# The last column chunk of a trunk's final GEMM cut into 384 and 128 tokens, the short piece in two feature halves

## The chip, the core and the metric

One core of a Trainium2 chip runs the kernel. Its engines work side by side, each in its own program order: TensorE (PE: matrix products into PSUM banks; PEld is its weight load), VectorE (DVE), ScalarE (ACT), GpSimd (POOL) and SyncE (SP), which here issues the DMAs. An instruction waits on semaphores for what it needs, and everything behind it on its engine or queue waits with it. The metric is device time in microseconds. A difference is told from no change when it is over 0.2%.

## The reference

Two layers run on 512 tokens of 2048 features in float32, a pooling mixer and then a sparse attention, each with adaLN shift, scale and gate; then one RMSNorm. What matters here is the end of layer 1 and what follows it:

```
mod = cond @ mod_w[i] + mod_b[i]
shift, scale, gate = jnp.split(mod, 3, axis=-1)
h = rms_norm(x, norm_g[i]) * (1.0 + scale[:, None, :]) + shift[:, None, :]
...
return (o * jax.nn.silu(gate)) @ w_out      # dsa_branch: output projection, 2048 x 2048
...
x = x + gate[:, None, :] * out
return rms_norm(x, final_g)                 # mean of squares over all 2048 features of a token
```

A token can only be normalised when all of its 2048 output features exist.

## The kernel before, in words

Activations are kept with features on the 128 partitions and tokens along the free dimension: a GEMM makes 128 features by up to 512 tokens in one PSUM bank. Each float32 product is made of three matmuls on fp32r halves: weight high by activation high, weight high by activation low, weight low by activation high (lines 191 to 193).

Weights come in units. `unit` (lines 143 to 151) has SP load a unit of 256 input rows by 512 output features into `st` (512 KB, three buffers), ACT cast it to the high half `wh` (L148, three buffers), and DVE subtract to get the low half `wl` (L150, three buffers). A `st` buffer comes free when its subtraction is done, a `wh` or `wl` buffer when TensorE has used it. `next_unit` keeps up to three units begun ahead of use, in the order of the list `plan`.

`gemm_t` (L178) goes over eight units (2048 input rows); for each it goes over four blocks of 128 features, two halves of the unit's rows, and the three products, so 24 matmuls a unit and 192 for a 512-feature chunk. In the last unit it calls `evac` for each block. After each unit it may run a hook (`mid`) and takes one item of the list `hot`.

The last GEMM (layer 1's `wout1`) has four chunks of 512 features. Chunks 0 to 2 take all 512 tokens at once. The last chunk is done in two pieces of tokens, 0 to 255 and 256 to 511, each with its own pass over the chunk's eight units (lines 1026 and 1027; line 977 lists them twice). The evacuation `out_evac` (L479 to L486) loads the residual `xr` (two buffers), forms the new `x2` on DVE (L481), squares it on ACT (L294), adds the square to `acc` on DVE (L295), and scales `x2` by `final_g` on ACT (L486). `norm_r` (L262) sums `acc` over the partitions with one-column matmuls (L266), and makes the reciprocal root (L269 to L280; the root on ACT, L271, loads an ACT table the first time). `fin_item` (L1005) then turns 128 tokens by 1024 features with eight TensorE transposes (L1013) into two banks, scales one bank on ACT (L1016) and the other on DVE (L1018), and has SP store both, 256 KB each (L1020; eight `fin` buffers). Eight items make the output: four for each token piece.

PSUM has eight banks: four named `acc`, three `att` and one `misc`; `bank()` (L90) deals out the first two names in turn. A scheduler lays the program's instructions out for each engine, mostly in program order; how they stand there is shown below.

Of the kernel before, what the change touches and what calls it, by code (L numbers as in the profile page):

```python
# [18 lines left out]
T = 512  # L19
# [33 lines left out]
def trunk(ctx, tc, xT, cols, crow, pos, modT, win, wgrp, wout0, widx, wgate, wqkv, wout1, out):  # L53
# [65 lines left out]
    hot = deque()  # L119
# [36 lines left out]
    plan = [(win[c, kp], 512) for k0, k1 in groups for c in chunks for kp in range(k0, k1)]  # L156
# [18 lines left out]
        nc.vector.tensor_tensor(lo, src, hi.bitcast(F32), op=OP.subtract)  # L175


    def gemm_t(kps, rhs, new_bank, evac, t0=0, t1=T, nstep=1, nhot=1, mid={}):  # L178
        banks = []
        for n, kp in enumerate(kps):  # L180
            wh, wl = next_unit()
            for m in range(4):
                if n == 0:
                    banks.append(new_bank())
                o = banks[m][:, 0:t1 - t0]
                for kk in range(2):
                    rh, rl = rhs(2 * kp + kk)
                    ms = slice(m * 128, m * 128 + 128)
                    first = n == 0 and kk == 0
                    last = n == len(kps) - 1 and kk == 1  # L190
                    mm(o, wh[:, kk, ms], rh[:, t0:t1], start=first, stop=False)  # L191
                    mm(o, wh[:, kk, ms], rl[:, t0:t1], start=False, stop=False)  # L192
                    mm(o, wl[:, kk, ms], rh[:, t0:t1], start=False, stop=last)  # L193
                if n == len(kps) - 1:
                    evac(m, o)
            if n in mid:
                mid[n]()
            step(nstep, nhot)
# [63 lines left out]
    def norm_r(t0, t1):  # L262
        nb = (t1 - t0) // 128
        p = misc()
        for j in range(nb):
            mm(p[:, j:j + 1], P["acc"][:, t0 + j * 128:t0 + j * 128 + 128], ones[:, 0:1], start=True, stop=True)  # L266
        s = P["tp"].tile([128, 4, 4], F32, name="nrm", tag="nrm", bufs=2)
        v, r, u, iv = (s[:, a, 0:nb] for a in range(4))
        nc.vector.tensor_scalar(v, p[:, 0:nb], 1.0 / D, EPS, op0=OP.mult, op1=OP.add)  # L269
        nc.vector.reciprocal(iv, v)  # L270
        nc.scalar.activation(r, iv, AF.Sqrt)  # L271
        refine(r, u, v)
        return r
# [177 lines left out]
    yT = {}  # L451
    while hot:
        hot.popleft()()
    for g in range(4):
        pooled = {}
        for kk in range(4):
            k = 4 * g + kk
# [14 lines left out]
    def out_evac(i, c, t0, t1, keep):  # L472
        def evac(m, o):
            mt = 4 * c + m
            if ("g", i, mt) not in done:
                ensure(("g", i, mt))
            xr = P["tp"].tile([128, T], F32, name="xr", tag="xr", bufs=2)
            n = t1 - t0
            nc.sync.dma_start(xr[:, 0:n], (xT if i == 0 else x1d)[mt][:, t0:t1])  # L479
            dst = keep(mt, t0, t1)  # L480
            nc.vector.scalar_tensor_tensor(dst, o, Gc[:, i, mt:mt + 1], xr[:, 0:n], op0=OP.mult, op1=OP.add)  # L481
            if i == 0:
                nc.sync.dma_start(x1d[mt][:, t0:t1], dst)
            add_square(dst, t0, t1, mt == 0)
            if i == 1:
                nc.scalar.activation(dst, dst, AF.Copy, scale=fg[:, mt:mt + 1])  # L486
        return evac
# [37 lines left out]
    for t0, hooks in ((0, {}), (256, {0: a0, 2: b0})):  # L525
        for c in (2, 3):
            gemm_t(range(8), lambda k: yT[k], bank, out_evac(0, c, t0, t0 + 256, keep0), t0, t0 + 256,
                   nstep=0, nhot=NH0, mid=hooks if c == 2 else {})
    early, early_g = [], []
    gemm_t(range(8), lambda k: hT[k], bank, lambda m, o: early_g.append((m, o)), 0, 256, nstep=0, nhot=NH1,  # L530
           mid={0: a1, 2: b1_})
# [383 lines left out]
    yT = {}  # L915
# [58 lines left out]
    eq.close()  # L974
    ctx.enter_context(open_banks())
    ctx.enter_context(open_work("right"))
    plan += [(wout1[c, kp], 512) for c in (0, 1, 2, 3, 3) for kp in range(8)]
    gemm_t(range(8), lambda k: yT[k], bank4, lambda m, o: early.append((m, o)), nstep=2.6, nhot=2, mid={6: drain})
    drain()
    el.close()  # L980
# [17 lines left out]
        gemm_t(range(8), lambda k: yT[k], bank, out_evac(1, c, 0, T, keep1), nstep=1)  # L998
    fin = {}

    def fin_r(t0):
        fin[t0] = norm_r(t0, t0 + 256)


    def fin_item(t0, tt, hf):  # L1005
        def run():
            r = fin[t0]
            c0 = t0 + tt * 128
            for q in range(2):
                p = bank()  # L1010
                for kk in range(4):
                    k = 8 * hf + 4 * q + kk
                    nc.tensor.transpose(p[:, kk * 128:kk * 128 + 128], x2[k][:, c0:c0 + 128], ident)  # L1013
                f = op_.tile([128, 512], F32, name="fin", tag="fin", bufs=8)
                if q == 0:
                    nc.scalar.activation(f, p, AF.Copy, scale=r[:, tt:tt + 1])  # L1016
                else:
                    nc.vector.tensor_scalar(f, p, r[:, tt:tt + 1], None, op0=OP.mult)  # L1018
                f0 = hf * 1024 + q * 512
                nc.sync.dma_start(out[c0:c0 + 128, f0:f0 + 512], f)  # L1020
        return run

    def fin_items(t0):
        return [fin_item(t0, tt, hf) for tt in range(2) for hf in range(2)]

    gemm_t(range(8), lambda k: yT[k], bank, out_evac(1, 3, 0, 256, keep1), 0, 256, nstep=0)
    gemm_t(range(8), lambda k: yT[k], bank, out_evac(1, 3, 256, T, keep1), 256, T, nstep=0,
           mid={0: lambda: fin_r(0), 2: lambda: hot.extend(fin_items(0))})
    fin_r(256)
    hot.extend(fin_items(256))  # L1030
    drain()
    es.close()

# [46 lines left out]
```

## Time and profile before

| | |
|---|---|
| median of 3 runs | 1649.99 us (1649.84 to 1651.13) |
| profiled execution, its own time | 1649.42 us |
| its span, first to last instruction | 1647.7 us |
| TensorE busy in the span | 98% |
| granted TensorE clock, mean over the span | 0.998 |
| last chunk, tokens 0 to 255 | 1584.36 to 1606.12 us |
| last chunk, tokens 256 to 511 | 1606.12 to about 1632.28 us |
| from there to the end of the span | 15.4 us |

The profiled execution's own time is 1.7 us longer than its span. Times of rows are microseconds from the start of the span. A matmul's row begins when it starts; matmuls are pipelined, so the distance between two starts, and not the length of a row, is what one costs. DMA rows on SPq are issues; the data lands later.

### The profile page before, as it was taken

The numbers are of one execution on the slowest core, as the hardware profiler recorded it, in microseconds if no ns is written. First come the engines' busy times: TensorE is split into PE (matmuls) and PEld (weight loads), VectorE is DVE, ScalarE is ACT, GpSimd is POOL, SyncE is SP. The second block draws the span as 40 slices with busy tenths as digits, with TensorE's granted clock in tenths as the row PEclk, the third lists the DMA queues.
The fourth block names the chain that finished last, engine by engine and source line by source line (L and its number), as shares of the span: only waits on it lengthen the run. The fifth ranks groups of instructions, "written<-read, shape, count | busy, mean of one in ns | idle before, by whom it ended". The sixth has DMA issues, their size and how long they took to land.

```text
span 1647.7 us, 23827 instructions
## 1 busy us (share of the span) xinstructions
PE 1615.6 (98%) x8892; PEld 1458.4 (89%) x8892; DVE 1259.6 (76%) x2147; ACT 726.4 (44%) x1150; POOL 128.0 (8%) x238
## 2 busy tenths in 40 slices
PE   5999999999999999999999999999999999999997
PEld 3888888888889999998889999999999999988897
DVE  6899999999974689765796676667776777756864
ACT  5622221334323556453324555455545555544344
POOL 0000000000000000010002121121312213000000
PEclk9999999999999999999999999999999999999999
DMA  9888888543786776442347897886968778637954
GB/s 347 318 302 308 322 336 339 207 178 114 289 294 207 237 246 195 142 148 100 104 152 170 196 175 165 181 166 176 168 169 179 166 185 163 201 115 279 363 183 171
DMA packets 106533, 348.21 MB, mean 211 GB/s; under 512 B 11953, under 2 KB 20273, under 8 KB 94001
## 3 DMA queue, kind: packets, MB, share of 16 engines
q1 hardware_dynamic: 87986, 296.35, 51.4%
q0 software_dynamic: 18432, 50.34, 18.3%
q8 instruction: 70, 1.15, 0.3%
q14 instruction: 45, 0.37, 0.1%
HBM read 330.39 MB, written 16.25 MB: 210 GB/s over the span
## 4 chain that ended last, share of the span: by engine, by line
PE 88%; DVE 4%; issue 3%; DMA 2%; ACT 1%; POOL 1%; SPq 0%; DVEq 0%; POOLq 0%; ACTq 0%
PE acc L191 11%; PE acc L192 11%; PE acc L193 11%; PE att L192 6%; PE att L191 6%; PE att L193 6%; PE by L816 4%; PE by L817 4%; PE by L818 4%; PE bx L816 2%; PE bx L818 2%; PE bx L817 2%; PE bz L816 2%; PE bz L818 2%; PE bz L817 2%
## 5 line engine op out<-in xcount | busy, mean ns | idle before, releaser
L148 ACT CAST wh<-st 128x1024 fp32r<-128x1024 f32 (+1 forms) x232 | 236.1, 1018 | 489.8 <-PE acc L192 266.3
L150 DVE TENSOR_TENSOR wl<-st,wh 128x1024 fp32r<-128x1024 f32 (+1 forms) x232 | 274.0, 1181 | 143.9 <-ACT wh L148 141.3
L191 PE MATMUL acc<-hi,wh 128*128 128x512 f32 (+1 forms) x810 | 299.0, 370 | 0.0
L192 PE MATMUL acc<-lo,wh 128*128 128x512 f32 (+1 forms) x810 | 298.9, 369 | 0.0
L193 PE MATMUL acc<-hi,wl 128*128 128x512 f32 (+1 forms) x810 | 298.5, 369 | 0.0
L226 DVE SCALAR_TENSOR_TENSOR ms<-ms,cb 128x2048 f32<-128x2048 f32 x96 | 218.9, 2285 | 12.3 <-DMA ms<-modT 10.1
L192 PEld LDWEIGHTS acc<-lo,wh 128*128 128x128 f32 x810 | 152.7, 189 | 26.6 <-DVE lo L175 0.2
L191 PEld LDWEIGHTS acc<-hi,wh 128*128 128x128 f32 x810 | 152.6, 189 | 26.5 <-ACT hi L174 0.4
L193 PEld LDWEIGHTS acc<-hi,wl 128*128 128x128 f32 x810 | 152.5, 188 | 26.5 <-DVE wl L150 0.2
L175 DVE TENSOR_TENSOR qwl<-qx,qwh 128x768 fp32r<-128x768 f32 x128 | 122.0, 957 | 66.8 <-ACT qwh L174 64.2
L191 PE MATMUL att<-hi,wh 128*128 128x512 f32 (+1 forms) x406 | 148.2, 366 | 4.7 <-ACT hi L311 4.7
L174 ACT CAST qwh<-qx 128x768 fp32r<-128x768 f32 x128 | 106.7, 836 | 102.7 <-PE bz L818 37.3
L192 PE MATMUL att<-lo,wh 128*128 128x512 f32 (+1 forms) x406 | 148.5, 366 | 0.0
L193 PE MATMUL att<-hi,wl 128*128 128x512 f32 (+1 forms) x406 | 148.3, 365 | 0.0
L175 DVE TENSOR_TENSOR qwl<-qy,qwh 128x768 fp32r<-128x768 f32 x96 | 91.5, 956 | 50.6 <-ACT qwh L174 48.8
L174 ACT CAST qwh<-qy 128x768 fp32r<-128x768 f32 x96 | 79.8, 833 | 88.1 <-PE by L818 39.2
L741 POOL DMA_DIRECT2D qx<-wqkv x96 | 83.4, 872 | 433.8 <-DVE stt L870 199.5
L191 PEld LDWEIGHTS att<-hi,wh 128*128 128x128 f32 x406 | 76.5, 189 | 17.5 <-ACT hi L311 5.1
L816 PE MATMUL bx<-qwh,hi 128*128 128x384 f32 x256 | 89.1, 348 | 0.0
L192 PEld LDWEIGHTS att<-lo,wh 128*128 128x128 f32 x406 | 76.6, 189 | 13.4 <-DVE lo L312 0.7
L816 PE MATMUL by<-qwh,hi 128*128 128x384 f32 x256 | 88.1, 344 | 0.0
L193 PEld LDWEIGHTS att<-hi,wl 128*128 128x128 f32 x406 | 76.7, 189 | 12.5
(286 smaller groups left out, 3501.1 us busy)
## 6 DMA issues: line engine op xcount, KB each, us to landing
ms<-modT SPq DMA_DIRECT2D x96, 1024.0 KB, 6.8
st<-wout SPq DMA_DIRECT2D x88, 512.0 KB, 4.1
qx<-wqkv POOLq DMA_DIRECT2D x96, 384.0 KB, 5.9
st<-win SPq DMA_DIRECT2D x64, 512.0 KB, 4.8
qy<-wqkv SPq DMA_DIRECT2D x64, 384.0 KB, 3.5
st<-wgate SPq DMA_DIRECT2D x40, 512.0 KB, 3.5
qx<-wqkv SPq DMA_DIRECT2D x32, 384.0 KB, 3.5
qy<-wqkv POOLq DMA_DIRECT2D x32, 384.0 KB, 5.9
```

Source lines behind the costliest of these rows:

```text
L148: nc.scalar.copy(wh, st)
L150: nc.vector.tensor_tensor(wl, st, wh.bitcast(F32), op=OP.subtract)
L174: nc.scalar.copy(hi, src)
L175: nc.vector.tensor_tensor(lo, src, hi.bitcast(F32), op=OP.subtract)
L191: mm(o, wh[:, kk, ms], rh[:, t0:t1], start=first, stop=False)
L192: mm(o, wh[:, kk, ms], rl[:, t0:t1], start=False, stop=False)
L193: mm(o, wl[:, kk, ms], rh[:, t0:t1], start=False, stop=last)
L226: nc.vector.scalar_tensor_tensor(st, st, 1.0, cell["cb"], op0=OP.mult, op1=OP.mult, accum_out=dst)
L741: nc.gpsimd.dma_start(d[kp], blk(j, name, kp), accum_op=OP.add)
L816: mm(o, hi, wh[:, kk, :], start=first, stop=False, skip_group_check=not opens)
L817: mm(o, hi, wl[:, kk, :], start=False, stop=False, skip_group_check=not opens)
L818: mm(o, lo, wh[:, kk, :], start=False, stop=last, skip_group_check=not opens)
```

## The change

The last chunk is cut into tokens 0 to 383 and 384 to 511. The first piece keeps its pass over eight units of 512 features. The second piece is done in two passes, each over eight units of 256 features, with two feature blocks in each, so 12 matmuls a unit of 128 columns each. The units of the second piece are slices of the same array: 256 of 512 features, 256 KB a unit. The norm of the first piece is made in unit 6 of the first half; its six `fin` items run from unit 1 of the second half on, one a unit. After the second half come one norm over 128 tokens and two items.

```diff
--- before.py
+++ after.py
@@ -175,17 +175,18 @@
         nc.vector.tensor_tensor(lo, src, hi.bitcast(F32), op=OP.subtract)
 
 
-    def gemm_t(kps, rhs, new_bank, evac, t0=0, t1=T, nstep=1, nhot=1, mid={}):
+    def gemm_t(kps, rhs, new_bank, evac, t0=0, t1=T, nstep=1, nhot=1, mid={}, ms_=range(4)):
         banks = []
         for n, kp in enumerate(kps):
             wh, wl = next_unit()
-            for m in range(4):
+            for m in ms_:
                 if n == 0:
                     banks.append(new_bank())
-                o = banks[m][:, 0:t1 - t0]
+                o = banks[m - ms_[0]][:, 0:t1 - t0]
                 for kk in range(2):
                     rh, rl = rhs(2 * kp + kk)
-                    ms = slice(m * 128, m * 128 + 128)
+                    m0 = (m - ms_[0]) * 128
+                    ms = slice(m0, m0 + 128)
                     first = n == 0 and kk == 0
                     last = n == len(kps) - 1 and kk == 1
                     mm(o, wh[:, kk, ms], rh[:, t0:t1], start=first, stop=False)
@@ -974,7 +975,8 @@
     eq.close()
     ctx.enter_context(open_banks())
     ctx.enter_context(open_work("right"))
-    plan += [(wout1[c, kp], 512) for c in (0, 1, 2, 3, 3) for kp in range(8)]
+    plan += [(wout1[c, kp], 512) for c in (0, 1, 2, 3) for kp in range(8)]
+    plan += [(wout1[3, kp][:, :, 256 * q:256 * q + 256], 256) for q in range(2) for kp in range(8)]
     gemm_t(range(8), lambda k: yT[k], bank4, lambda m, o: early.append((m, o)), nstep=2.6, nhot=2, mid={6: drain})
     drain()
     el.close()
@@ -998,8 +1000,11 @@
         gemm_t(range(8), lambda k: yT[k], bank, out_evac(1, c, 0, T, keep1), nstep=1)
     fin = {}
 
+
+    cut = 384
+
     def fin_r(t0):
-        fin[t0] = norm_r(t0, t0 + 256)
+        fin[t0] = norm_r(t0, cut if t0 == 0 else T)
 
 
     def fin_item(t0, tt, hf):
@@ -1021,13 +1026,14 @@
         return run
 
     def fin_items(t0):
-        return [fin_item(t0, tt, hf) for tt in range(2) for hf in range(2)]
-
-    gemm_t(range(8), lambda k: yT[k], bank, out_evac(1, 3, 0, 256, keep1), 0, 256, nstep=0)
-    gemm_t(range(8), lambda k: yT[k], bank, out_evac(1, 3, 256, T, keep1), 256, T, nstep=0,
-           mid={0: lambda: fin_r(0), 2: lambda: hot.extend(fin_items(0))})
-    fin_r(256)
-    hot.extend(fin_items(256))
+        return [fin_item(t0, tt, hf) for tt in range(3 if t0 == 0 else 1) for hf in range(2)]
+
+    gemm_t(range(8), lambda k: yT[k], bank, out_evac(1, 3, 0, cut, keep1), 0, cut, nstep=0)
+    for q in range(2):
+        gemm_t(range(8), lambda k: yT[k], bank, out_evac(1, 3, cut, T, keep1), cut, T, nstep=0,
+               mid={1: lambda: hot.extend(fin_items(0))} if q else {6: lambda: fin_r(0)}, ms_=range(2 * q, 2 * q + 2))
+    fin_r(cut)
+    hot.extend(fin_items(cut))
     drain()
     es.close()
```

How the instructions move. The first place is SP's queue from the last full units of the last chunk to the end. `st<-wout` loads a weight unit, `xr<-x1d` a residual, `out<-fin` stores a result. Before:

```order
L146 DMA st<-wout 128x1024 x6
L479 DMA xr<-x1d 128x256
L146 DMA st<-wout 128x1024
L479 DMA xr<-x1d 128x256 x2
L146 DMA st<-wout 128x1024
L479 DMA xr<-x1d 128x256
L146 DMA st<-wout 128x1024 x2
L1020 DMA out<-fin 128x512 x4
L479 DMA xr<-x1d 128x256 x2
L1020 DMA out<-fin 128x512 x12
```

The same stretch of SP's queue with the change:

```order
L146 DMA st<-wout 128x1024 x2
L146 DMA st<-wout 128x2x256 x5
L480 DMA xr<-x1d 128x384 x2
L480 DMA xr<-x1d 128x128
L146 DMA st<-wout 128x2x256
L480 DMA xr<-x1d 128x128
L146 DMA st<-wout 128x2x256 x7
L480 DMA xr<-x1d 128x128 x2
L146 DMA st<-wout 128x2x256 x3
L1025 DMA out<-fin 128x512 x16
```

Eight full units became sixteen half units, some of them behind residual loads, and all sixteen stores now stand behind the last weight load.

The second place is ACT around the first norm's root. `CAST wh<-st` makes a unit's high half, `nrm` is the norm's small tile, `x_12` to `x_15` are the chunk's four feature blocks. Before:

```order
L294 ACTIVATE tmp<-x_15_14578 128x256
L486 ACTIVATE x_15_14578<-x_15_14578,cl 128x256
L148 CAST wh<-st 128x1024
L271 ACT_TABLE_LOAD
L271 ACTIVATE nrm<-nrm 128x2
L148 CAST wh<-st 128x1024
L1016 ACTIVATE fin<-acc,nrm 128x512
L148 CAST wh<-st 128x1024
L1016 ACTIVATE fin<-acc,nrm 128x512
```

With the change:

```order
L148 CAST wh<-st 128x512 x6
L272 ACT_TABLE_LOAD
L272 ACTIVATE nrm<-nrm 128x3
L295 ACTIVATE tmp<-x_12_14575 128x128
L487 ACTIVATE x_12_14575<-x_12_14575,cl 128x128
L148 CAST wh<-st 128x512
L295 ACTIVATE tmp<-x_13_14576 128x128
L487 ACTIVATE x_13_14576<-x_13_14576,cl 128x128
L148 CAST wh<-st 128x512 x2
L1021 ACTIVATE fin<-acc,nrm 128x512
L148 CAST wh<-st 128x512
L1021 ACTIVATE fin<-acc,nrm 128x512
```

The table load, the root and the first half's evacuation now stand between the casts of units 9 and 10 of the sixteen half units (counted from 0).

The third place is TensorE at the chunk's last six matmuls. `L191` to `L193` (`L192` to `L194` with the change) are the three products, `ident,x` is a transpose of one feature block. Before:

```order
L191 MATMUL att<-hi_14521,wh 128x256
L192 MATMUL att<-lo_14522,wh 128x256
L193 MATMUL att<-hi_14521,wl 128x256
L191 MATMUL att<-hi_14525,wh 128x256
L192 MATMUL att<-lo_14526,wh 128x256
L193 MATMUL att<-hi_14525,wl 128x256
L1013 MATMUL acc<-ident,x_0_14563 128x128
L1013 MATMUL acc<-ident,x_1_14564 128x128
L1013 MATMUL acc<-ident,x_2_14565 128x128
```

With the change:

```order
L192 MATMUL att<-hi_14521,wh 128x128
L193 MATMUL att<-lo_14522,wh 128x128
L194 MATMUL att<-hi_14521,wl 128x128
L192 MATMUL att<-hi_14525,wh 128x128
L193 MATMUL att<-lo_14526,wh 128x128
L194 MATMUL att<-hi_14525,wl 128x128
L1018 MATMUL att<-ident,x_0_14563 128x128
L1018 MATMUL att<-ident,x_1_14564 128x128
L1018 MATMUL att<-ident,x_2_14565 128x128
```

The last matmuls keep their number and lose half their columns. Of the 64 transposes, 24 stood among the matmuls before and 40 behind the last; now 48 stand among them and 16 behind.

## Rows read from the trace of the kernel before

**Rows 1.** The page: busy us, share of the span and instructions by engine.

```profile
PE 1615.6 (98%) x8892; PEld 1458.4 (89%) x8892; DVE 1259.6 (76%) x2147; ACT 726.4 (44%) x1150; POOL 128.0 (8%) x238
```

**Rows 2.** Windows: length, then busy PE, PEld, DVE, ACT, POOL, clock, DMA share, GB/s.

```profile
1584.36:1606.12 21.76, 21.76 (x193) 21.76 (x192) 12.94 (x15) 11.90 (x15) 0.00 (x0) 1.00 0.60 200
1606.12:1632.28 26.16, 25.40 (x222) 25.11 (x221) 13.61 (x24) 13.15 (x21) 0.00 (x0) 1.00 0.45 146
1632.28:1641.21 8.93, 5.73 (x46) 4.72 (x44) 6.58 (x15) 5.55 (x11) 0.00 (x0) 1.00 0.50 180
1641.21:1647.70 6.49, 0.00 (x0) 0.00 (x0) 0.00 (x1) 0.00 (x0) 0.00 (x0) 0.55 0.71 256
```

**Rows 3.** Timeline (start, length, engine, line): the last chunk's last matmul.

```profile
1632.17 0.28 PE L193 MATMUL att<-hi,wl 128*128 128x256 f32 x1
```

**Rows 4.** Timeline, 384-column matmuls back to back, twelve starts from first to last.

```profile
1406.94 0.33 PE L816 MATMUL bz<-qwh,s4h 128*128 128x384 f32 x1
...
1408.85 0.34 PE L818 MATMUL bz<-qwh,s4l 128*128 128x384 f32 x1
```

**Rows 5.** Timeline, matmuls of 64 columns (five starts) and of 128 columns.

```profile
629.02 0.28 PE L214 MATMUL acc<-wl,hi 128*128 128x64 f32 x1
...
629.25 0.28 PE L213 MATMUL acc<-wh,hi 128*128 128x64 f32 x1
629.36 0.28 PE L214 MATMUL acc<-wl,hi 128*128 128x64 f32 x1
629.47 0.28 PE L215 MATMUL acc<-wh,lo 128*128 128x64 f32 x1
...
1342.67 0.22 PE L894 MATMUL att<-ph,vh 128*128 128x128 f32 x1
1342.73 0.28 PE L895 MATMUL att<-pl,vh 128*128 128x128 f32 x1
1342.84 0.27 PE L896 MATMUL att<-ph,vl 128*128 128x128 f32 x1
```

**Rows 6.** Timeline, eight transposes of one item and the matmul behind them.

```profile
1615.77 1.04 PE L1013 MATMUL acc<-ident,x 128*128 128x128 f32 x8
1616.56 0.36 PE L191 MATMUL acc<-hi,wh 128*128 128x256 f32 x1
```

**Rows 7.** Groups by line and shape: count, busy us, mean ns, idle before.

```profile
L174 ACT CAST hi<-pv 128x512 fp32r<-128x512 f32 x16 | 9.9, 620 | 18.4 <-DVE pv L415 15.4 <-PE att L193 2.8
L175 DVE TENSOR_TENSOR lo<-pv,hi 128x512 fp32r<-128x512 f32 x16 | 10.7, 682 | 0.0
L271 ACT ACT_TABLE_LOAD x1 | 1.3, 1283 | 0.0
```

**Rows 8.** DMA issues from 1584.36 us (KB, us to landing); then `fin` stores alone.

```profile
st<-wout SPq DMA_DIRECT2D x11, 512.0 KB, 3.5
xr<-x1d SPq DMA_DIRECT2D x8, 128.0 KB, 2.5
...
L1020 SPq DMA_DIRECT2D out<-fin x16: 332/384/1135, 1617.5 to 1643.1; - x16
DMA to landing us min/median/max: 2.3/3.0/4.5
```

**Rows 9.** Timeline of the end: last evacuation, norm, first and last scaling.

```profile
1635.18 0.48 DVE L481 SCALAR_TENSOR_TENSOR x<-att,Gc,xr 128x256 f32<-128x256 f32 x1
1636.14 0.42 DVE L295 TENSOR_TENSOR acc<-acc,tmp 128x256 f32<-128x256 f32 x1 [0.48 <-ACT tmp L294]
1636.62 0.61 PE L266 MATMUL misc<-ones,acc 128*128 128x1 f32 x4
1637.27 0.16 DVE L269 TENSOR_SCALAR nrm<-misc 128x2 f32<-128x2 f32 x1 [0.70 <-PE misc L266]
1638.48 0.75 DVE L1018 TENSOR_SCALAR fin<-acc,nrm 128x512 f32<-128x512 f32 x1
...
1640.47 0.74 DVE L1018 TENSOR_SCALAR fin<-acc,nrm 128x512 f32<-128x512 f32 x1
```

## The prediction

> **What bounds the kernel now.** I read the page first: TensorE is busy 98% of the span [rows 1]. A stage that adds TensorE work therefore adds time, except where TensorE stands idle. Next I cut the end of the span into windows at the starts of the last chunk's pieces and at its last matmul [rows 2, 3]. The reader is to see three regimes. The first token piece takes 21.76 us and TensorE is busy for all of it. The second takes 26.16 us and TensorE is busy for 25.4. It ends a matmul's step after the last start, at 1632.17 + 0.11 = 1632.28. From there to the end of the span, 15.4 us, TensorE only turns tokens, and in the last 6.5 us no engine computes: stores land. So the change pays in the first two windows and can earn only in the last two. [...]
>
> **What a matmul costs by its columns.** I took starts from the timeline where matmuls run back to back. 384 columns: (1408.85 - 1406.94) / 11 = 0.1736 us [rows 4]. 256 columns: 21.76 / 192 = 0.1133 us [rows 2]. For 128 columns the kernel has no long stream, so I bound it. Five starts of 64 columns lie (629.47 - 629.02) / 4 = 0.1125 us apart, no less than 256 columns cost [rows 5]; what runs under a short matmul is the load of the next 128x128 weights, and that sets the step. The few matmuls of 128 columns show one step of 0.06 us and then 0.11 us [rows 5]: the first one's weights were loaded under a long matmul before it, the next ones' were not. The two around the short step also share their weights (`vh`), as one neighbouring pair in three will in the changed piece; but the five starts of 64 columns have such a pair among them too (L213 and L214, both `hi`) and no short step. The bounds are thus 0.06 and 0.1125 us; I take 0.1125, since in the changed piece every matmul stands behind a short one.
>
> [...]
>
> **The change part by part.**
>
> *First piece, 384 columns.* The same 192 matmuls, each longer: 192 x 0.1736 = 33.3 us against 21.76, so +11.6 us. TensorE is the bound in that window, and a unit of weights now lasts 4.2 us there instead of 2.7, so no weights come late; nothing hides or adds to this.
>
> *Second piece, 128 columns in two halves.* Still 192 matmuls: 192 x 0.1125 = 21.6 us. Half the columns thus save 0.2 us where one would look for 11: that is the point of this prediction. Between the matmuls now stand six items of eight transposes instead of three items' worth (48 instead of 24); eight take 1616.56 - 1615.77 = 0.79 us [rows 6], so 6 x 0.79 = 4.7 us. The first norm's matmuls take some 0.4 us (four rows take 0.61 [rows 9], here there are three). Without waits the piece takes 26.7 us against 26.16: +0.6 us.
>
> *Waits that this piece gains.* A unit now lasts 12 x 0.1125 = 1.35 us on TensorE instead of 24 x 0.1133 = 2.72, and three `st` buffers must follow. (a) One round of a buffer is landing, cast and subtraction. A 128 KB load lands in 2.5 us and a 512 KB one in 3.5 [rows 8], so 3.0 for 256 KB; cast and subtraction of 128x512 take 0.62 and 0.68 [rows 7]; with 0.2 for handovers that is 4.5 us for three units, 1.5 a unit. Five half units stand ahead of the residuals on SP and are loaded under the first piece, and from unit 9 on the transposes make a unit last 1.35 + 0.79 = 2.14 us, so only units 5 to 8 run on the ring: 4 x 0.15 = 0.6 us. (b) On ACT the table load (1.28 us [rows 7]), the root and the first half's square and scale stand ahead of unit 10's cast, about 2.2 us in all; TensorE has unit 9 and eight transposes to do meanwhile, 2.14 us, but then needs cast and subtraction, of which I count 0.8 us as seen. (c) The second half holds two of the three `att` banks to its end, so the third and fourth items pass through the one that is left, each waiting for a scaling of some 0.75 us [rows 9]; two waits of 0.4 us. Together 2.2 us. Below: 0, if the units stay ahead. Above: with the longest landing of the stores, 4.5 us [rows 8], a round is 6.0 us, 2.0 a unit, so 4 x 0.65 = 2.6, with all of (b) 2.2 and two full scalings 1.5: 6.3 us. I take 2.2, because landing lies between two measured neighbours. The piece then costs +2.8 us.
>
> *The end.* Before, 15.4 us. After, from the last matmul: 0.2 us until its result is there; the last evacuation, 1636.56 - 1635.18 = 1.4 us for 256 columns [rows 9], 1.1 for 128; the norm's matmul for one block, 0.5 (0.65 for two); from L269 to the first scaling 1638.48 - 1637.27 = 1.2 us [rows 9], which does not shrink, being six small instructions in a chain; two scalings on each engine in place of four, 2 x 0.75 = 1.5 us. That is 4.5 us. Then the stores. Before, the last scaling ended at 1641.21 and the last store was issued at 1643.1 [rows 8, 9], behind others in SP's queue, and the span ended 4.6 us after that. After, four stores are left, of which two follow the last scaling; I take 0.7 us to the last issue and 3.0 to land: 3.7 us. The end is 8.2 us, so -7.2 us. Bounds: 6.7 us (landing in 2.3, evacuation in 0.7) and 11.6 us (the stores as slow as before, 6.5). The residuals of the last two blocks are issued ahead of the last three weight units, so the last evacuation does not wait for them; the twelve earlier stores are issued behind the last weight load, at about unit 11, and have some 10 us.
>
> **The sum.** +11.6 + 2.8 - 7.2 = +7.2 us. On the profiled execution's 1649.42 us that gives 1656.6; the median of the runs lies 0.6 higher, so I predict 1657.2 us.
>
> **The rivals.**
>
> *Weights come late* (0.13). The half units are 1 KB runs of an array of 2 KB rows, and a small load is not much quicker than a large one (128 KB and 512 KB differ by 1.0 us [rows 8]). If landing is 4.5 us, waits reach the 6.3 us above: +11.3, 1661.3 us. Against it: in the second piece DMA was busy only 0.45 of the time [rows 2].
>
> *Stores crowd the end* (0.06). Sixteen stores wait behind the last weight load. 3 MB of the first twelve at the 256 GB/s that the stores reached [rows 2] is 12.3 us; if they start no earlier than 8 us before the last matmul, the last four land behind them as before: the end is 11.6 us, the sum +10.6, 1660.6 us. Against it: the first of them can start while unit 11 runs, five units of 2.14 us ahead of the last matmul, and some 4 us more pass before the last scalings.
>
> *A short matmul is cheaper in a stream* (0.05). What speaks for it is the one step of 0.06 us [rows 5]. If short and long steps alternate, the mean is 0.085 us and TensorE saves 192 x 0.0275 = 5.3 us. The ring's 1.5 us a unit stays, so only the second half saves its share: 8 x 12 x 0.0275 = 2.6: 7.2 - 2.6 = +4.6; with no waits for weights at all it is 7.2 - 2.2 - 5.3 = -0.3, no change. Between the two I put 1652 us.
>
> [...]
>
> *Faster after all* (0.03). The same mechanism carried through: every step is 0.06 us and units arrive as fast as they are used. The short piece saves 192 x 0.0525 = 10.1 us, and the waits vanish: 7.2 - 2.2 - 10.1 = -5.1, 1644.9 us. It decides from a step of 0.086 us down, where 192 times the saving equals the 5.0 us that are left without waits. Against it: PE has as many weight loads as matmuls [rows 1], and the stream of 64 columns holds its 0.1125 us [rows 5].
>
> **How the numbers follow.** The forecast has 0.73. Its own range, from no waits and a short end to some more of both, is 1653.5 to 1661. The range takes in part of the first two rivals: 1652.5 to 1662. 0.2% is 3.3 us, about what a measurement can tell here. Faster by more than that is the last rival, 0.03; within it lies the third and the forecast's lowest edge, 0.05; slower has 0.92.
>
> **What would show it.** In the changed profile: the first piece's window near 33.3 us; 128-column starts 0.11 us apart, near 0.06 if I am wrong; the second piece 28 to 30 us, with TensorE idle before units 6 and 10 and at the third and fourth items; from the last matmul to the end 8 to 9 us. A second piece under 24 us, or an end over 11 us, would make the prediction wrong in its terms; 1653 us or less would make it wrong in its size.

## The result and the profile after

The changed kernel takes 1662.68 us in the median of six runs (1659.35 to 1664.61); before, beside it, 1650.04 us. The ratio is 1.0073, 95% interval 1.0063 to 1.0083: slower, as predicted, but by 12.6 us in place of 7.2, and 0.7 us above the range. The profiled execution has 1661.85 us and a span of 1660.0. Ratios here and below compare runs in the same state, so one run of the one-pass kernel below, 2023.47 us at a mean clock of 0.754, is left out of its ratio.

Windows of the changed kernel, cut as in [rows 2]: the piece of 384 tokens, the piece of 128, the evacuation and scaling behind it, the last landing.

```profile
1583.18:1617.10 33.92, 33.92 (x193) 33.91 (x192) 13.43 (x17) 12.32 (x17) 0.00 (x0) 1.00 0.35 113
1617.10:1650.57 33.47, 32.80 (x248) 32.32 (x247) 17.97 (x34) 17.25 (x31) 0.00 (x0) 0.85 0.53 179
1650.57:1655.20 4.63, 2.38 (x20) 1.90 (x19) 3.06 (x10) 2.85 (x7) 0.00 (x0) 0.96 0.31 116
1655.20:1660.00 4.80, 0.00 (x0) 0.00 (x0) 0.00 (x0) 0.00 (x0) 0.00 (x0) 0.50 0.60 219
```

Against [rows 2] that is 33.92 - 21.76 = +12.2 us, 33.47 - 26.16 = +7.3 and 9.43 - 15.42 = -6.0; the last chunk starts 1.2 us earlier. Sum +12.3 us, the difference of the spans. The clock of the short piece is 0.85, where every window that computes had 1.00 before. The same piece cut where the clock changes:

```profile
1617.10:1627.12 10.02, 9.73 (x85) 9.54 (x85) 6.19 (x10) 6.03 (x11) 0.00 (x0) 1.00 0.42 140
1627.12:1627.50 0.38, 0.38 (x6) 0.38 (x5) 0.13 (x1) 0.22 (x1) 0.00 (x0) 1.00 0.31 43
1627.50:1637.80 10.30, 10.30 (x51) 10.30 (x50) 5.13 (x15) 5.75 (x11) 0.00 (x0) 0.50 0.53 165
1637.80:1650.57 12.77, 12.39 (x112) 12.11 (x111) 6.51 (x10) 5.25 (x9) 0.00 (x0) 1.00 0.61 226
```

For 10.3 us the granted clock is 0.50, though TensorE is busy through all of them. This stretch is called the fall below. The step of a matmul is 0.21 us in it and 0.112 ahead of it, so the same work would have taken about half as long: some 5 us are lost. Of the other five runs only the mean clock is on record. Such a stretch takes 0.003 off the mean of 1660 us. The timeline of TensorE (start, length, line; in brackets the idle time before it) shows what came before:

```profile
1625.39 0.27 PE L193 MATMUL acc<-lo,wh 128*128 128x128 f32 x1
1625.95 0.33 PE L194 MATMUL acc<-hi,wl 128*128 128x128 f32 x1 [0.29 <-DVE wl L150]
...
1626.34 0.27 PE L194 MATMUL acc<-hi,wl 128*128 128x128 f32 x1
...
1627.01 0.28 PE L194 MATMUL att<-hi,wl 128*128 128x128 f32 x1
1627.12 0.98 PE L267 MATMUL misc<-ones,acc 128*128 128x1 f32 x6
...
1628.22 0.41 PE L193 MATMUL acc<-lo,wh 128*128 128x128 f32 x1
1628.43 0.41 PE L194 MATMUL acc<-hi,wl 128*128 128x128 f32 x1
1628.64 0.41 PE L192 MATMUL acc<-hi,wh 128*128 128x128 f32 x1
...
1635.68 1.93 PE L1018 MATMUL acc<-ident,x 128*128 128x128 f32 x8
```

The reader sees ten microseconds of 128-column matmuls, a wait for weights (unit 6), the six one-column matmuls of the first norm, and from there a step of 0.21 us where it was (1627.01 - 1626.34) / 6 = 0.112. The step at full clock is the upper bound that the prediction took from [rows 5]. The row of the first item's eight transposes is 1.93 us long, not the 1.04 of [rows 6].

The end on the timeline, beside [rows 9]:

```profile
1650.46 0.28 PE L194 MATMUL att<-hi,wl 128*128 128x128 f32 x1
...
1651.08 0.34 DVE L482 SCALAR_TENSOR_TENSOR x<-att,Gc,xr 128x128 f32<-128x128 f32 x1
...
1653.78 0.75 DVE L1023 TENSOR_SCALAR fin<-att,nrm 128x512 f32<-128x512 f32 x1
1654.44 0.74 DVE L1023 TENSOR_SCALAR fin<-acc,nrm 128x512 f32<-128x512 f32 x1
```

The stores by their line (count, issue from first to last, time to landing):

```profile
L1025 SPq DMA_DIRECT2D out<-fin x16: 332/333/611, 1637.7 to 1655.9; - x16
...
DMA to landing us min/median/max: 2.2/2.7/3.9
```

The last scaling ends 1655.18 - 1650.57 = 4.6 us behind the last matmul (4.5 predicted). The last store is issued 0.7 us later, as assumed, but the span ends 4.1 us after that, not 3.0. The slowest of the sixteen landings is 3.9 us; before, the slowest was 4.5 [rows 8], and the span ended 4.6 us after the last issue.

### The profile page after: what moved, and what is told of

It is laid out like the page before. It is cut to its first block, busy times and chain, and to the rows that moved or that the text cites. A ratio compares the mean times of both kernels' runs of the same rounds, so it can differ in the third digit from the quotient of the medians.

```text
span 1660.0 us, 23874 instructions
## 1 busy us (share of the span) xinstructions
PE 1630.9 (98%) x8892; PEld 1474.2 (89%) x8892; DVE 1261.0 (76%) x2155; ACT 727.9 (44%) x1158; POOL 128.0 (8%) x238
## 4 chain that ended last, share of the span: by engine, by line
PE 96%; DVE 2%; ACT 1%; DMA 1%; issue 1%; POOL 0%; DVEq 0%; SPq 0%; ACTq 0%; POOLq 0%
PE acc L192 12%; PE acc L194 12%; PE acc L193 12%; PE att L194 6%; PE att L193 6%; PE att L192 6%; PE by L817 4%; PE by L819 4%; PE by L818 4%; PE bz L817 3%; PE bz L819 3%; PE bz L818 3%; PE bx L817 3%; PE bx L819 3%; PE bx L818 3%; PE att L884 1%
## 5 line engine op out<-in xcount | busy, mean ns | idle before, releaser
L148 ACT CAST wh<-st 128x1024 fp32r<-128x1024 f32 (+2 forms) x240 | 237.6, 990 | 506.5 <-PE acc L193 277.1
L150 DVE TENSOR_TENSOR wl<-st,wh 128x1024 fp32r<-128x1024 f32 (+2 forms) x240 | 275.5, 1148 | 162.1 <-ACT wh L148 159.8
L194 PE MATMUL acc<-hi,wl 128*128 128x512 f32 (+3 forms) x810 | 301.7, 373 | 0.4 <-DVE wl L150 0.3
L192 PE MATMUL acc<-hi,wh 128*128 128x512 f32 (+3 forms) x810 | 301.9, 374 | 0.0
L193 PE MATMUL acc<-lo,wh 128*128 128x512 f32 (+3 forms) x810 | 301.8, 373 | 0.0
L227 DVE SCALAR_TENSOR_TENSOR ms<-ms,cb 128x2048 f32<-128x2048 f32 x96 | 219.0, 2286 | 11.6 <-DMA ms<-modT 9.6
L194 PEld LDWEIGHTS acc<-hi,wl 128*128 128x128 f32 x810 | 152.6, 189 | 27.4 <-DVE wl L150 0.9
L192 PEld LDWEIGHTS acc<-hi,wh 128*128 128x128 f32 x810 | 152.8, 189 | 26.6 <-ACT hi L174 0.4
L193 PEld LDWEIGHTS acc<-lo,wh 128*128 128x128 f32 x810 | 152.8, 189 | 26.5 <-DVE lo L175 0.2
L192 PE MATMUL att<-hi,wh 128*128 128x512 f32 (+3 forms) x406 | 150.6, 372 | 4.7 <-ACT hi L312 4.7
L193 PE MATMUL att<-lo,wh 128*128 128x512 f32 (+3 forms) x406 | 150.8, 371 | 0.0
L194 PE MATMUL att<-hi,wl 128*128 128x512 f32 (+3 forms) x406 | 150.6, 371 | 0.0
L192 PEld LDWEIGHTS att<-hi,wh 128*128 128x128 f32 x406 | 78.2, 193 | 17.6 <-ACT hi L312 5.1
L193 PEld LDWEIGHTS att<-lo,wh 128*128 128x128 f32 x406 | 78.3, 193 | 13.3 <-DVE lo L313 0.7
L194 PEld LDWEIGHTS att<-hi,wl 128*128 128x128 f32 x406 | 78.2, 193 | 12.5
```

Source lines behind the costliest of these rows:

```text
L148: nc.scalar.copy(wh, st)
L150: nc.vector.tensor_tensor(wl, st, wh.bitcast(F32), op=OP.subtract)
L227: nc.vector.scalar_tensor_tensor(st, st, 1.0, cell["cb"], op0=OP.mult, op1=OP.mult, accum_out=dst)
```

## The experiments

Three theories, my guesses, stood at the start. A: the 128-column matmuls leave TensorE so sparse that the granted clock falls. B: the wait for weights and the one-column matmuls of the norm bring it down. C: the clock is a side matter, and the halved units come too late. All kernels below are edits of the changed one; the kernel before ran beside each of them (medians 1650.85 to 1651.24 us). Each has a trace of one run. Of its other runs only the time and the mean clock are known, and the mean tells less than a trace: the kernel before, without any 128-column stream, has 0.996 to 0.998 beside the experiments.

### Padding the short matmuls to 256 columns

```diff
-        gemm_t(range(8), lambda k: yT[k], bank, out_evac(1, 3, cut, T, keep1), cut, T, nstep=0,
+        ev3 = out_evac(1, 3, cut, T, keep1)
+        gemm_t(range(8), lambda k: yT[k], bank, lambda m, o: ev3(m, o[:, 128:256]), 256, T, nstep=0,
```

> The changed kernel, but each matmul of the short piece streams 256 columns (tokens 256 to 511); only the last 128 are evacuated, so 128 columns of each are computed for nothing and the output is the same. Theory A (the granted clock falls to 0.50 because a 128-column matmul leaves TensorE's columns half empty beside the weight load that sets its step): the step stays 0.113 us, the clock stays at 1.00 through the whole short piece, which takes about 28.5 us in place of 33.5; the mean granted clock is back at 0.998, and the time is 1657 to 1658 us against 1662.7, although more is computed. Theory B (the stall for weights near unit 6 and the one-column matmuls of the first norm make the clock fall): both stand where they stood, so the clock falls to 0.50 for some 10 us again, 1662 us. Theory C (no matter what the clock, half units come late): the second piece stays above 31 us with waits for weights in the trace.

1659.57 us, ratio 1.0049 (1.0037 to 1.0061); the mean clock is 0.999 in all five runs. Its three windows:

```profile
1584.49:1617.77 33.28, 33.28 (x193) 33.27 (x192) 13.44 (x17) 12.27 (x17) 0.00 (x0) 1.00 0.36 114
1617.77:1647.03 29.26, 28.58 (x247) 28.01 (x247) 17.51 (x34) 16.54 (x32) 0.00 (x0) 1.00 0.63 208
1647.03:1656.30 9.27, 2.36 (x20) 1.88 (x18) 3.05 (x10) 2.74 (x7) 0.00 (x0) 0.89 0.46 170
```

Its norm and its wait for weights on the timeline:

```profile
1627.30 0.72 PE L267 MATMUL misc<-ones,acc 128*128 128x1 f32 x6
...
1633.53 0.39 PE L194 MATMUL att<-hi,wl 128*128 128x256 f32 x1 [0.20 <-DVE wl L150]
```

The short piece computes twice as much and takes 29.3 us in place of 33.5, at a clock of 1.00. The one-column matmuls are in it and bring nothing down. The wait for weights is in it too, but 6 us behind the norm and not 1.2 us ahead of it, so this run does not repeat the wait and the norm in a row. What it shows is that the columns matter: B falls as far as the one-column matmuls alone go, and C falls. The time is 2 us above what A expected.

### One pass, without halves

```diff
-    plan += [(wout1[c, kp], 512) for c in (0, 1, 2, 3) for kp in range(8)]
-    plan += [(wout1[3, kp][:, :, 256 * q:256 * q + 256], 256) for q in range(2) for kp in range(8)]
+    plan += [(wout1[c, kp], 512) for c in (0, 1, 2, 3, 3) for kp in range(8)]
...
+    gemm_t(range(8), lambda k: yT[k], bank, out_evac(1, 3, cut, T, keep1), cut, T, nstep=0,
+           mid={0: lambda: fin_r(0), 2: lambda: hot.extend(fin_items(0))})
```

> The token pieces of 384 and 128 alone: the short piece in one pass over 512-feature units, norm after unit 0, the items of the first piece from unit 2 on, as the kernel before has them. Theory A: the 128-column matmuls are the same 192, now with 8 transposes after each of units 2 to 7; the clock falls to 0.50 some 10 us into the short piece, or sooner or later, and costs about 5 us of it. The end has four features blocks' evacuations behind the last matmul in place of two, some 1 us more than the 9.4 us of the changed kernel. About 1662 us. Theory B: the one-column matmuls of the norm come at unit 0 already, so the fall would start there, near the beginning of the short piece. Theory C: no wait for weights here, the piece near 27.5 us, 1657 to 1658 us.

Ratio 1.0148 (1.0119 to 1.0177), the costliest of all, with clocks of 0.985 to 0.994 in the five runs compared. Windows: to the norm, the norm's first 0.54 us, and what follows.

```profile
1619.96:1625.26 5.30, 2.79 (x25) 2.65 (x24) 3.96 (x6) 3.93 (x8) 0.00 (x0) 1.00 0.66 254
1625.26:1625.80 0.54, 0.54 (x5) 0.54 (x5) 0.00 (x0) 0.54 (x2) 0.00 (x0) 0.98 0.87 281
1625.80:1639.40 13.60, 13.60 (x66) 13.60 (x65) 5.01 (x9) 4.67 (x6) 0.00 (x0) 0.50 0.30 88
```

```profile
1625.26 1.00 PE L267 MATMUL misc<-ones,acc 128*128 128x1 f32 x6 [2.51 <-DVE acc L296]
```

I had not expected that the norm after unit 0 waits 2.5 us for the evacuation of 384 columns. Behind that wait and the norm the clock falls early, as B's sentence has it, and for 13.6 us in place of 10.3. The longer interruption went with the longer fall; how much of the time is the fall, and how much the wait itself and the longer end, is not taken apart here.

### Halves alone, cut at 256

```diff
-    cut = 384
+    cut = 256
```

The items are then two blocks a piece. The first norm stands after unit 6 of the first half, as in the changed kernel (its rows begin at 1614.46 us, ahead of the second half), and not inside the second half, as the expectation below has it.

> The two feature halves alone: the cut is at 256 tokens as before, the second piece of 256 tokens runs in two halves of its features, the first norm inside the second half. Theory A: all matmuls have 256 columns or more, so no fall of the clock, 0.998. A unit of half the features takes 12 x 0.113 = 1.36 us as in the changed kernel, so the waits for weights, if any, show here alone. The second piece 25.5 to 28 us, the end about 3 us shorter than the 15.4 us before since the halved last unit leaves two evacuations instead of four: 1647 to 1651 us. Theory B: the stall and the one-column matmuls are here too; the clock falls for some 10 us, 1653 to 1656 us. Theory C: waits for weights of 3 us and more in the second piece, 1651 to 1654 us.

1649.93 us, ratio 0.9993 (0.9983 to 1.0004): no change that can be told. The clock is at 0.998 or 0.999 in ten of eleven runs.

```profile
1582.87:1604.62 21.75, 21.75 (x193) 21.75 (x192) 12.45 (x16) 10.85 (x15) 0.00 (x0) 1.00 0.47 152
1604.62:1632.71 28.09, 27.34 (x230) 26.34 (x229) 16.95 (x34) 15.77 (x31) 0.00 (x0) 1.00 0.66 215
1632.71:1645.60 12.89, 4.56 (x38) 3.84 (x36) 4.78 (x12) 4.36 (x9) 0.00 (x0) 0.85 0.45 164
```

Halving costs the second piece 28.09 - 26.16 = 1.9 us and takes 15.42 - 12.89 = 2.5 us off the end. In the second piece the norm and a wait for weights (0.23 us) stand among matmuls of 256 columns, and the clock holds. The cost of the change lies in the cut at 384.

### The norm later in the stream

```diff
-               mid={1: lambda: hot.extend(fin_items(0))} if q else {6: lambda: fin_r(0)}, ms_=range(2 * q, 2 * q + 2))
+               mid={1: lambda: fin_r(0), 2: lambda: hot.extend(fin_items(0))} if q else {}, ms_=range(2 * q, 2 * q + 2))
```

> The changed kernel with the first norm's one-column matmuls after unit 1 of the second half in place of unit 6 of the first, and the items from unit 2 of the second half on. Theory A: the clock still falls near the same place, some 10 us into the short piece (1627.5), since the stream of 128-column matmuls ahead of it is the same, and with no one-column matmul before it; 1662 to 1664 us. Theory B in its form that the one-column matmuls make it fall: it holds 1.00 until they come, 4 us or more later, or does not fall: 1657 to 1660 us.

1659.2 us, ratio 1.0054 (1.0042 to 1.0066); two runs of five have a lower clock (0.996, 1662.8 and 1663.0 us), three have not (0.998 to 1.000, 1658.1 to 1659.2 us). Windows of the profiled one, which is one of the two, to the norm, the norm, and the fall:

```profile
1618.26:1632.76 14.50, 14.11 (x122) 13.69 (x121) 8.38 (x15) 7.77 (x15) 0.00 (x0) 1.00 0.49 153
1632.76:1633.50 0.74, 0.74 (x9) 0.74 (x9) 0.39 (x1) 0.71 (x3) 0.00 (x0) 0.98 0.70 126
1633.50:1643.70 10.20, 10.20 (x50) 10.16 (x50) 5.38 (x13) 5.34 (x9) 0.00 (x0) 0.50 0.57 184
```

Its wait for weights:

```profile
1627.21 0.33 PE L194 MATMUL acc<-hi,wl 128*128 128x128 f32 x1 [0.29 <-DVE wl L150]
```

In this trace the fall moved with the one-column matmuls: A as I had it, with no part for the norm, is wrong here. Behind that wait the clock holds for 5.5 us more, until the norm. From this came theory D: one-column matmuls behind a stream of 128-column ones bring the clock down.

### The norm with 128 columns of ones

```diff
-            mm(p[:, j:j + 1], P["acc"][:, t0 + j * 128:t0 + j * 128 + 128], ones[:, 0:1], start=True, stop=True)
+            mm(p[:, j * w:j * w + w], P["acc"][:, t0 + j * 128:t0 + j * 128 + 128], ones[:, 0:w], start=True, stop=True)
...
-        fin[t0] = norm_r(t0, cut if t0 == 0 else T)
+        fin[t0] = norm_r(t0, cut if t0 == 0 else T, 128 if t0 == 0 else 1)
```

> The changed kernel, but the first norm's matmuls in the short piece have 128 equal columns of ones in place of one; the result is read from one column of each block. Their place, weights and waits are the same. Theory D (new, from the earlier runs: what makes the granted clock fall is the row of one-column matmuls that follows a stream of 128-column ones): the clock stays at 1.00 through the short piece in all runs, mean 0.999, about 1658 to 1659 us. Theory A (the stream of 128-column matmuls by itself makes it fall): it falls in the short piece as in the changed kernel in most runs, 0.995 to 0.997 and 1661 to 1664 us.

1660.28 us, ratio 1.0056 (1.0043 to 1.0069). Five runs of six hold 0.998 or 0.999 (1658.3 to 1661.4 us), one has 0.995 and 1665.4 us, though its norm has no one-column matmul. The interval overlaps that of the changed kernel (1.0063 to 1.0083), so the gain itself is not clear of noise. The profiled run is the changed kernel without a fall; its windows and its waits on TensorE in the short piece:

```profile
1583.93:1617.85 33.92, 33.92 (x193) 33.92 (x192) 13.43 (x17) 12.32 (x17) 0.00 (x0) 1.00 0.35 115
1617.85:1647.37 29.52, 27.84 (x247) 27.41 (x247) 17.67 (x34) 16.89 (x31) 0.00 (x0) 1.00 0.63 203
1647.37:1656.80 9.43, 2.38 (x20) 1.90 (x19) 3.05 (x10) 2.84 (x7) 0.00 (x0) 0.75 0.46 168
```

```profile
PE att L1018 <- ACT fin L1021: 1.4, 1, 1.4
PE acc L194 <- DVE wl L150: 0.3, 1, 0.3
```

Without the fall the short piece takes 29.5 us where I had predicted 28 to 30. This stream, too, holds matmuls of 128 columns, a wait for weights and the norm's rows, and yet the clock held.

### The norm and the items out of the stream

```diff
-               mid={1: lambda: hot.extend(fin_items(0))} if q else {6: lambda: fin_r(0)}, ms_=range(2 * q, 2 * q + 2))
+               ms_=range(2 * q, 2 * q + 2))
+    fin_r(0)
+    hot.extend(fin_items(0))
```

> The changed kernel without the first norm and the items of the first piece in the stream: both come after the last matmul. Theory D: no one-column matmul in the stream of 128-column ones, so the clock stays at 1.00 until the stream ends; the short piece is 192 matmuls without transposes, 21.6 us and about 0.5 us of waits for weights. Theory A: the clock falls inside the stream, which then takes 26 us or more. The end is longer in both, since all 48 transposes of the first piece, their scalings and their stores stand there: 3 MB more to store at about 256 GB/s, some 10 us more than the 9.4 us of the changed kernel, so 1662 to 1666 us by D and 1667 to 1671 us by A.

1669.5 us, ratio 1.0112 (1.0098 to 1.0127), clocks 0.993 or 0.994 in all four runs. Windows of the stream to the fall, of its rest, and of the norm and transposes behind it; then the timeline ahead of the fall:

```profile
1619.04:1636.60 17.56, 16.88 (x142) 16.11 (x142) 9.96 (x18) 9.57 (x20) 0.00 (x0) 1.00 0.51 150
1636.60:1647.50 10.90, 10.90 (x53) 10.90 (x53) 3.40 (x6) 2.73 (x6) 0.00 (x0) 0.50 0.23 70
1647.50:1653.40 5.90, 5.90 (x31) 5.90 (x31) 2.63 (x15) 3.37 (x8) 0.00 (x0) 0.50 0.00 0
```

```profile
1633.72 0.33 PE L192 MATMUL att<-hi,wh 128*128 128x128 f32 x1 [0.22 <-ACT wh L148]
...
1634.45 0.33 PE L194 MATMUL att<-hi,wl 128*128 128x128 f32 x1 [0.29 <-DVE wl L150]
...
1636.62 0.41 PE L192 MATMUL att<-hi,wh 128*128 128x128 f32 x1
```

The clock falls with no one-column matmul in the stream, so D falls too. But two waits for weights stand 2 to 3 us ahead of the fall. Four shorter ones, steps of 0.20 to 0.41 us ahead of a matmul on `wl`, stand between 1623 and 1632 us. Either the stream suffices, or the waits take the norm's part.

### A stream with nothing in between, and the padded one with its waits

The first is the kernel with the norm out of the stream, but in one pass of whole units, with the plan as in the one pass above:

```diff
-    for q in range(2):
...
+    gemm_t(range(8), lambda k: yT[k], bank, out_evac(1, 3, cut, T, keep1), cut, T, nstep=0)
+    fin_r(0)
+    hot.extend(fin_items(0))
```

> The pieces of 384 and 128 in one pass of 512-feature units, the first norm and its items after the last matmul: 192 matmuls of 128 columns in a row, with whole units whose weights have 2.7 us each, so no waits, no one-column matmuls and no transposes among them. If the stream of 128-column matmuls by itself brings the granted clock down (theory A in its plain form): it falls to 0.50 at the latest some 17 to 20 us into the piece, as with the norm at the end in halves, mean 0.993 to 0.995. If the two short waits for weights that came 2 to 3 us before that fall were needed (theory B again): the piece runs through in 21.6 us at 1.00; a fall after its end, where TensorE waits and transposes, speaks for neither.

1661.86 us, ratio 1.0064 (1.0049 to 1.0079), a mean clock of 0.998 in all four runs. The 192 matmuls (with two more rows at the edges):

```profile
1617.80:1639.19 21.39, 21.39 (x194) 21.39 (x193) 11.05 (x15) 10.07 (x16) 0.00 (x0) 1.00 0.36 120
```

The second is the kernel with the norm out of the stream, in halves, and padded with the two lines of the first experiment; behind the loop stands:

```diff
+    fin_r(0)
+    hot.extend(fin_items(0))
```

> The changed kernel with the first norm and its items after the last matmul, and each matmul of the short piece streaming 256 columns, of which the last 128 are evacuated: 128 columns of each are computed for nothing. Weights and waits as with the norm at the end and 128 columns. Theory A: the clock stays at 1.00 to the last matmul, the piece takes about 22.3 us in place of some 28, and the time falls from 1669.5 to about 1663 us. Theory B (the short waits for weights bring it down): it falls late in the stream again, 1669 us.

1664.54 us, ratio 1.0085 (1.0067 to 1.0103); three runs of four have 0.998, one 0.996 with no trace of it (1668.2 us). The profiled one has two waits for weights in the piece, 0.51 and 0.23 us, and no fall:

```profile
1619.71:1644.06 24.35, 23.49 (x194) 22.81 (x194) 12.86 (x23) 11.43 (x23) 0.00 (x0) 1.00 0.47 139
```

So A in its plain form is wrong: 192 matmuls of 128 columns in a row, without a wait, kept the full clock. And the waits alone are not it either: in the padded trace the clock stays at 1.00 behind them, and they cost the piece time alone, 24.4 us where 192 steps of 0.1133 are 21.8. In the short piece every traced fall had both ahead of it, matmuls of 128 columns and an interruption among them. Both together are not enough to make one: the trace of the norm with 128 columns has both without a fall. The kernel without waits also differs from the one with them in its units, 512 and not 256 features, so the waits are not the only difference there.

### Many one-column matmuls behind 256-column ones

```diff
-    cut = 384
+    cut = 256
...
-            mm(p[:, j:j + 1], P["acc"][:, t0 + j * 128:t0 + j * 128 + 128], ones[:, 0:1], start=True, stop=True)
+            for _ in range(reps):
+                mm(p[:, j:j + 1], P["acc"][:, t0 + j * 128:t0 + j * 128 + 128], ones[:, 0:1], start=True, stop=True)
```

The first norm has six repetitions, the second one.

> The cut at 256 tokens with the second piece in two halves, and the first norm's one-column matmuls, after unit 6 of the first half, done six times over (24 rows in the trace in place of 4; 20 are for nothing). Theory D: if the one-column matmuls by themselves make the clock fall, it falls behind 256-column matmuls too, near the end of these 24 rows, to 0.50 for some 10 us, 1656 us; if it takes 128-column matmuls ahead of them, the clock stays at 1.00 and the time is that of the halves at 256 and 20 x 0.12 = 2.4 us, 1652 us. Theory A: no fall, 1652 us.

1650.98 us, ratio 1.0002 (0.9993 to 1.001), clocks 0.997 to 0.999. The windows of the 24 one-column rows, the next 0.5 us, and the fall:

```profile
1615.10:1617.90 2.80, 2.80 (x27) 2.80 (x26) 0.72 (x2) 1.22 (x3) 0.00 (x0) 1.00 0.79 239
1617.90:1618.40 0.50, 0.50 (x6) 0.50 (x6) 0.47 (x3) 0.50 (x1) 0.00 (x0) 1.00 0.79 260
1618.40:1621.60 3.20, 3.20 (x18) 3.20 (x17) 2.33 (x8) 1.86 (x6) 0.00 (x0) 0.50 0.41 116
```

With 24 of them in place of 4 the clock falls behind long matmuls too, so 128-column matmuls are not a condition everywhere. But among 256-column matmuls it is back after 3.2 us; in the kernels with 128-column ones the falls of the profiled runs lasted 10 to 17 us. The expectation of some 10 us was not met.

### Stores of the last piece from two queues

The halves at 256, to see whether the shorter end can be had for good:

```diff
-                nc.sync.dma_start(out[c0:c0 + 128, f0:f0 + 512], f)
+                (nc.scalar if q == 0 and t0 else nc.sync).dma_start(out[c0:c0 + 128, f0:f0 + 512], f)
```

> The cut at 256 tokens with the second piece in two halves, the first norm after unit 6 of the first half, items from unit 1 of the second half, and the stores of the last piece's ScalarE results issued from ScalarE's queue in place of SyncE's. If the end is bound by SyncE's queue of stores, it gets 1 us shorter than the 12.9 us of the halves at 256: 1648 to 1649 us. If it is bound by the chain of norm, scalings and the landing of the last store, nothing changes: 1649.9 us; and if issuing delays ScalarE's scalings it is up to 1 us longer.

1649.15 us, ratio 0.9992 (0.9984 to 1.0001): nothing that can be told. The end in its trace:

```profile
1638.25:1651.00 12.75, 4.55 (x38) 3.83 (x36) 4.77 (x12) 4.47 (x9) 0.00 (x0) 0.81 0.45 166
```

That is 12.75 us against 12.89, so SyncE's queue is not its bound. The mean clock of the traced run is 0.997, though each 5 us from 1580 to 1645 us of its trace has 1.00: a mean of 0.997 by itself does not tell a fall in the short piece. No version here is shown to beat the kernel before.

## Why the prediction was right and wrong

**The sign held, and so did the mechanism, the price of half the columns.** "192 x 0.1125" for half the columns: the step is 0.112 us at full clock, in a stream of 21.39 / 192 = 0.111. Both rivals with a cheaper short matmul fall. In the changed kernel's trace the weight loads start just as far apart, (1626.95 - 1626.06) / 8 = 0.111 us; that they set the step is my inference, and no run takes it apart.

**The step that failed** is that the sum has no term for the clock. It was built on the windows before, which have 1.00 where TensorE computes [rows 2] but hold no stream of 128 columns. In the profiled run the clock is at 0.50 for 10.3 us of the short piece, which takes 33.47 us with this fall and 29.52 without it (the norm with 128 columns): about 4 us. A fall costs some 5 us of matmuls, and the waits give part of it back: TensorE idles 0.7 us in the short piece with the fall, 1.7 us without. Of the six runs, five have a mean clock of 0.995 to 0.997 and take 1661.9 to 1664.6 us; the one at 0.999 took 1659.35, inside the range. That the four without a trace fell in the same place is inferred from this, least surely for the one at 0.997. Padding, which keeps the mean at 0.999 in all runs, takes 3 us off the median.

**The waits, +2.8 predicted for the second piece.** With the clock held, 29.52 - 26.16 = +3.4. In place of 0.6 for the ring, one wait of 0.3 (between starts 0.45: a step of 0.56 in place of 0.11); in place of 0.8 for the table load, none; in place of 0.8 for the bank, 1.4 in one wait. These idle times are 1.7 us, not 2.2. TensorE's own work, 26.7 us in the prediction, is 27.84: among other things the prediction read the first norm as three rows in 0.4 us, where the trace has six, two for each block, in 0.63. The sum was close, the parts were not, so that much of the closeness is luck.

**The first piece, +11.6 predicted:** +12.2, because the step was 0.1767 us (33.92 / 192) and not the 0.1736 of [rows 4].

**The end, -7.2 predicted:** -6.0. I took a median landing for the last store, 3.0 us, but the span ended 4.1 us after the last issue, near the slowest landing, 3.9. The two bounds of the prediction do not follow from its terms: 4.5 - 0.4 + 0.7 + 2.3 is 7.1 us and not 6.7, and 4.5 + 6.5 is 11.0 and not 11.6, which makes "Stores crowd the end" 1660.0 us. The 9.4 us measured lie inside either pair.

In the profiled run the terms miss by +0.6 us (first piece), +4.5 (second piece) and +1.2 (end), and an earlier start of the last chunk, for which no cause is shown, gives 1.2 back: 7.2 + 5.1 = 12.3. Without the fall, in the run with the wide norm, it is -0.4 (an earlier start) + 12.2 + 3.4 - 6.0 = +9.1 us on the profiled span, its 1656.8 us, and that lies inside the range. So the fall, the largest miss, is what takes the median over the edge: the runs with the lower clock lie from 1661.85 us, just under 1662, up to 1664.61, and the other misses alone do not reach it. "Weights come late", which forecast 1661.3, came near the time for another reason: the one wait for weights is 0.3 us, though it stands ahead of the fall.

What stays open: what exactly brings the clock down. The same kernel has a lower clock in some runs and not in others (five of six of the changed kernel, two of five with the norm late, one of six with the wide norm), and the runs do not say what differs between them.

## What to carry to other kernels

A shorter matmul buys nothing below a step that does not shrink with its columns: here 128 columns took 0.112 us and 256 took 0.1133. Read the step in the trace before cutting columns. The clock was lost too in most of the traces: of the five here with waits or a norm's matmuls in a stream of 128 columns, four have a fall to 0.50, of 10 to 17 us, and one has none. Here the same halves with a cut at 256 tokens kept the clock in the profiled run and changed the time by nothing that can be told (0.9993); padding the cut at 384 to 256 columns regained part of its loss (1.0049 against 1.0073). And price the end by the slowest landing, not the median: in the traces before and after, the span ended 4.6 and 4.1 us after the last store's issue, with slowest landings of 4.5 and 3.9 us and medians of 3.0 and 2.7.

## What the runs showed of the hardware

In the changed kernel's trace the granted clock was at 0.50 for 10.3 us with TensorE busy in all of them. In another trace 192 matmuls of 128 columns in a row, without a wait, kept it at 1.00 for 21.4 us. A kernel that computes more was quicker than one that computes less (1659.57 against 1662.68 us). In the first piece the same 192 matmuls had a step of 0.1767 us in the traces of five kernels (33.92 us) and of 0.1733 in three (33.28 us in the padded one), at a clock of 1.00 in every window read there; why isn't settled.
